# Adding up indexer heads: 128x32 weight matrices on TensorE in place of weighted adds on VectorE and GpSimd

## The chip, the cores and the metric

The kernel is one launch on one core of a Trainium2 chip. The metric is the device time of that launch in microseconds (us); the kernel before ran three times, and its median is 3490.73 us. TensorE (PE) multiplies matrices into the accumulation memory (PSUM); VectorE (DVE), ScalarE (ACT) and GpSimd (POOL) work element by element; SyncE (SP) issues transfers (DMA), which ACT can issue too. Each engine carries out its own instructions in order, and waits for others by semaphores.

## The reference

One decoder layer over 2048 tokens of width 1024. The mixer has two branches that share the input and output projections: sparse attention, whose keys an indexer selects, and an RWKV-7 recurrence. A SwiGLU feed-forward part follows. The change concerns the indexer. Cut to what matters:

```
def block(i):                    # 128 queries
    score = einsum('bth,bths->bts', wi, relu(einsum('bthd,bsd->bths', qi, ik)))   # 8 heads of 64
    score = where(s_pos <= t_pos, score, -inf)
    _, sel = top_k(score, 256)
    ...                          # attention over the selected keys, with a relative bias
```

So for each query and each earlier key, 8 head products go through a relu, are weighted by a number per query and head (`wi`), and are added.

## The kernel before

Four phases follow each other: `phase_in` (projections, to about 769 us), `phase_scan` (to about 1407), `phase_att` (to about 1925) and `phase_ffn`.

`phase_in` works on four groups of 512 tokens. Its function `job` makes the query products of the indexer (`iq`), and of attention (`q`, `k`), as a high and a low half of fp32r, and stores them to DRAM by 256-KB DMAs on SP.

`phase_scan` records two lists of steps into one another. The main list is the RWKV scan: 32 chunks of 64 tokens, for which `load`, `load_t` and `load_r` read matrices from DRAM (BK, ARV, TT, IR), and whose ticks end in an update of the state (L1626, L1627). The side list is the selection (`select_steps`): it takes the query blocks 2 to 15 in five units, (15, 10), (14, 11), (13, 12), (9, 8, 7) and (6, 5, 4, 3, 2). In unit u's span of the scan its scores are made, in u+1's a threshold for the 256 best is searched, in u+2's the mask is written. If a check finds a wrong count, a repair branch runs on DVE. The spans' widths stand in a table (`SPANS`), and each side step gets a position in its span (`at`); a scheduler then orders the instructions of each engine.

The scores of one block are made in pieces of up to 512 keys: 38 pieces in all, 25 of 512 columns, 7 of 384 and 6 of 256. For each piece and each of the 8 heads, `score` multiplies 128 queries of one head by the keys' high half (L933) and low half (L934) into one of two banks `sc`, and ACT takes the relu (L937). Then the heads are added up: head 0 is weighted by POOL into `acc` (L939), head 1 weighted and added by POOL (L941, L942), and heads 2 to 7 each by one DVE instruction (L944):

```
nc.vector.scalar_tensor_tensor(acc[:, ks], r[:, 0:n], w, acc[:, ks], op0=OP.mult, op1=OP.add)
```

`start` loads the indexer's keys `ik` (L873) and weights `iwT` (L876) on SP, ACT and POOL split the keys in two halves (L881, L882), and 16 transposes turn the weights (L885). `others` makes the table of the attention's relative bias: one f32 matmul (L901) gives 8 rows of 384, and one DMA (L911) writes each row 128 times to DRAM (`toep`, 1536 KB). These steps are issued at the scan's start, among the first loads of the scan on SP: `load(0)` (L1529, L1530) ahead of them, the TT loads (L1540, L1541) around them.

Of the kernel before, what the change touches and what calls it, by code (L numbers as in the profile page):

```python
# [144 lines left out]
def phase_in(e, c_in, ada_w, ada_b, x, w_in, pre_gain, q_norm, kv_norm, idx_k_norm,  # L145
# [9 lines left out]
    with ExitStack() as ctx:  # L155
# [289 lines left out]
        def job(g, b, st):  # L445

            gsl = slice(g * G, (g + 1) * G)
            if b in ("iq", "q", "k"):
# [30 lines left out]
            elif b == 3:  # L479
# [4 lines left out]
                nc.sync.dma_start(d.iwT[:, gsl], t[96:104])  # L484
# [325 lines left out]
BESIDE = 2  # L810
# [31 lines left out]
def select_steps(e, pool, psum, ps_, ranks, rel_bias, onehot, d):  # L842
# [19 lines left out]
    iww = pool.tile([P, NB, H], F32, name="iww", bufs=1)  # L862
# [6 lines left out]
    def start():  # L869

        raw = pool.tile([P, UW], F32, name="acc", bufs=3)[:, 0:T]
        for s in (lo, hi):
            nc.sync.dma_start(raw[s], d.ik)  # L873
        wide = pool.tile([P, T], F32, name="xm", bufs=1)
        iwr = wide[0:H]
        nc.sync.dma_start(iwr, d.iwT)  # L876
# [7 lines left out]
        for b in range(NB):  # L884
            nc.tensor.transpose(tp[:, b * H:(b + 1) * H], iwr[:, b * P:(b + 1) * P], e.ident[0:H, 0:H])  # L885
        nc.vector.tensor_scalar(iww.rearrange("p a h -> p (a h)"), tp[:, 0:NB * H], float(8 ** -0.5 * 64 ** -0.5), None, op0=OP.mult)

    def others():
# [22 lines left out]
        nc.sync.dma_start(d.toep, t[:, None, :].to_broadcast([H, P, 384]))  # L911
# [10 lines left out]
    def queries(b):  # L922

        q = pool.tile([P, H, P], F32R, name="iqs", bufs=2)
        for i, s in enumerate((lo, hi)):
            nc.sync.dma_start(f32(q[s]), d.iqT[i, :, b * P:(b + 1) * P].rearrange("(h x) t -> x h t", h=H))
        qs[b] = q

    def score(b, h, o, n):
        acc = accs[b]  # L930
        sp = psum.tile([P, G], F32, name="sc", bufs=2)
        ks = slice(o, o + n)
        nc.tensor.matmul(sp[:, 0:n], qs[b][:, h, :], ikh[:, ks], start=True, stop=False)  # L933
        nc.tensor.matmul(sp[:, 0:n], qs[b][:, h, :], ikl[:, ks], start=False, stop=True)  # L934
        w = iww[:, b, h:h + 1]
        r = pool.tile([P, G], F32, name="relu2", bufs=2) if h < BESIDE else pool.tile([P, G], F32, name="relu", bufs=3)
        nc.scalar.activation(r[:, 0:n], sp[:, 0:n], AF.Relu)  # L937
        if h == 0:
            nc.gpsimd.tensor_tensor(acc[:, ks], r[:, 0:n], w.to_broadcast([P, n]), op=OP.mult)  # L939
        elif h < BESIDE:  # L940
            nc.gpsimd.tensor_tensor(r[:, 0:n], r[:, 0:n], w.to_broadcast([P, n]), op=OP.mult)  # L941
# [1357 lines left out]
```

## Time and profile before

| | us |
|---|---|
| median of 3 runs (lowest, highest) | 3490.73 (3482.89, 3492.33) |
| profiled execution, its span | 3490.94, 3489.2 |
| phase_in: 0 to 769, PE busy | 684.57 |
| gap at the scan's start: 769 to 794, PE busy | 5.07 |
| scores beside the scan: 790 to 1300, PE, DVE, ACT, POOL busy | 421.02, 429.36, 342.59, 259.99 |
| phase_att: 1407 to 1925, PE busy | 480.72 |
| phase_ffn: 1925 to 3489, PE busy | 1510.58 |

PE is busy for 91% of the span, and the phases after the scan are PE's almost alone. The scan stage is the one in which DVE, ACT and POOL have as much to do. A PE record's end is modelled: consecutive matmuls overlap in the records, so the pitch from one start to the next tells what one costs, and not its length. The granted clock (PEclk) is a share of 2.4 GHz.

### The profile page before, as it was taken

Reading aid. Unit: us, or ns where it says so; the run is one execution under the profiler, and the core shown is the slowest. Engines: PE = TensorE matmul, PEld = TensorE weight load, DVE = VectorE, ACT = ScalarE, POOL = GpSimd, SP = SyncE. Lnnn points to the kernel's source line nnn. Section 1 sums busy time; section 2 is a strip of 40 time slices with the busy share of each in tenths; the row PEclk is TensorE's granted clock in tenths of the full one; section 3 lists DMA queues with packets and bytes.
Section 4 is the critical chain, followed back from the end, with each engine's and each line's share of the span. In section 5 each row is a group of like instructions: output and inputs, shape, how many; then the busy total and the mean of one; then the engine's idle time right before and its main releaser. Section 6 shows DMA issues by size and latency. Waiting matters only on the chain.

```text
span 3489.2 us, 47343 instructions
## 1 busy us (share of the span) xinstructions
PE 3186.4 (91%) x15940; PEld 2529.9 (73%) x15940; DVE 2403.5 (69%) x4736; ACT 1758.5 (50%) x3261; POOL 815.4 (23%) x818
## 2 busy tenths in 40 slices
PE   5989999987886898699999898999999989999998
PEld 4666667665675777487877686888887878888886
DVE  5558585765998888488888445786567576656556
ACT  3535353435775776476666443533336443333444
POOL 3545555544554544221110121000000000000000
PEclk8999999987987889799999899999999999999999
DMA  7465747375322343773341477594338653333665
GB/s 203 128 174 140 189 122 214 90 200 114 80 73 69 96 104 98 171 171 85 96 107 39 128 243 272 182 313 138 100 124 291 196 171 109 97 100 109 201 194 194
DMA packets 643431, 516.79 MB, mean 148 GB/s; under 512 B 219520, under 2 KB 509088, under 8 KB 643040
## 3 DMA queue, kind: packets, MB, share of 16 engines
q1 hardware_dynamic: 643176, 513.67, 50.5%
q8 instruction: 126, 2.06, 0.2%
q14 instruction: 129, 1.06, 0.1%
HBM read 355.37 MB, written 158.17 MB: 147 GB/s over the span
## 4 chain that ended last, share of the span: by engine, by line
PE 44%; DVE 5%; DMA 5%; issue 2%; ACT 2%; SPq 1%; POOL 0%; POOLq 0%; DVEq 0%; ACTq 0%
PE b L77 10%; PE b L78 10%; PE b L79 10%; PE pt L1367 3%; PE o L78 2%; PE s L1328 2%; PE o L77 2%; PE o L79 1%; PE s L1329 1%; DMA fb<-hT 1%; PE om L79 1%; DVE wp L1874 1%; PE om L78 1%; PE om L77 1%; DMA fx<-in_w_ffn_down_dram 1%
## 5 line engine op out<-in xcount | busy, mean ns | idle before, releaser
L77 PE MATMUL b<-hT,wp 128*128 128x512 f32 x704 | 276.7, 393 | 4.9 <-ACT wp L1873 3.2
L78 PE MATMUL b<-hT,wp 128*128 128x512 f32 x704 | 276.0, 392 | 0.0
L79 PE MATMUL b<-hT,wp 128*128 128x512 f32 x704 | 275.1, 391 | 0.0
L403 POOL TENSOR_TENSOR wl<-wr,wh 128x512 fp32r<-128x512 f32 (+1 forms) x154 | 203.5, 1338 | 265.6 <-ACT wh L402 260.9
L1873 ACT ACTIVATE wp<-fwr 128x512 fp32r<-128x512 f32 x286 | 177.4, 622 | 165.2 <-PE b L79 91.3
L1874 DVE TENSOR_TENSOR wp<-fwr,wp 128x512 fp32r<-128x512 f32 x286 | 195.9, 686 | 90.9 <-ACT wp L1873 89.7
L77 PE MATMUL b<-wp 128*128 128x512 f32 x616 | 240.1, 390 | 8.5 <-ACT wp L1873 8.5
L78 PE MATMUL b<-wp 128*128 128x512 f32 x616 | 241.7, 392 | 1.7 <-DVE wp L1874 1.4
L77 PE MATMUL mm<-hh,wh 128*128 128x512 f32 (+1 forms) x576 | 241.2, 423 | 1.6 <-ACT wh L402 1.2
L79 PE MATMUL b<-wp 128*128 128x512 f32 x616 | 241.1, 391 | 0.0
L78 PE MATMUL mm<-hl,wh 128*128 128x512 f32 (+1 forms) x576 | 235.0, 408 | 1.3 <-POOL hl L208 1.0
L79 PE MATMUL mm<-hh,wl 128*128 128x512 f32 (+1 forms) x576 | 233.8, 406 | 2.0 <-POOL wl L403 2.0
L1370 ACT ACTIVATE ph<-pt 128x512 fp32r<-128x512 f32 x272 | 158.5, 593 | 123.9 <-PE pt L1367 103.7
L1874 DVE TENSOR_TENSOR wp<-po,wp 128x512 fp32r<-128x512 f32 x154 | 106.3, 691 | 162.5 <-ACT wp L1873 162.4
L1371 DVE TENSOR_TENSOR pl<-pt,ph 128x512 fp32r<-128x512 f32 x272 | 183.9, 687 | 44.3 <-ACT ph L1370 42.9
L77 PE MATMUL b<-hB,wp 128*128 128x512 f32 x528 | 208.4, 395 | 2.5 <-ACT wp L1873 2.5
L79 PE MATMUL b<-hB,wp 128*128 128x512 f32 x528 | 207.9, 394 | 1.5 <-DVE wp L1874 1.5
L78 PE MATMUL b<-hB,wp 128*128 128x512 f32 x528 | 208.1, 394 | 0.0
L944 DVE SCALAR_TENSOR_TENSOR acc<-relu,iww,acc 128x512 f32<-128x512 f32 (+2 forms) x228 | 175.3, 774 | 37.2 <-ACT relu L937 32.0
L937 ACT ACTIVATE relu<-sc 128x512 f32<-128x512 f32 (+2 forms) x304 | 158.3, 542 | 83.0 <-PE sc L934 58.6
L1346 ACT ACTIVATE pr<-pr,nmx 128x1024 f32<-128x1024 f32 (+7 forms) x192 | 171.2, 894 | 55.8 <-DVE nmx L1343 55.3
L933 PE MATMUL sc<-ikh,iqs 128*128 128x512 f32 (+2 forms) x304 | 146.6, 483 | 54.3 <-ACT relu L937 52.2
(504 smaller groups left out, 8459.8 us busy)
## 6 DMA issues: line engine op xcount, KB each, us to landing
wr<-in_w_in_dram SPq DMA_DIRECT2D x63, 512.0 KB, 3.9
fwr<-in_w_ffn_gate_dram SPq DMA_DIRECT2D x44, 512.0 KB, 3.9
fwr<-in_w_ffn_up_dram SPq DMA_DIRECT2D x44, 512.0 KB, 3.9
po<-act_S SPq DMA_DIRECT2D x88, 256.0 KB, 2.7
fwr<-dT SPq DMA_DIRECT2D x88, 256.0 KB, 3.5
act_A<-po SPq DMA_DIRECT2D x66, 256.0 KB, 2.0
act_S<-fb SPq DMA_DIRECT2D x66, 256.0 KB, 2.0
fwr<-in_w_ffn_down_dram SPq DMA_DIRECT2D x66, 256.0 KB, 3.4
```

Of the source, the lines that this page charges most:

```text
L77: nc.tensor.matmul(out, lh, rh, start=first, stop=False, skip_group_check=more)
L78: nc.tensor.matmul(out, lh, rl, start=False, stop=False, skip_group_check=more)
L79: nc.tensor.matmul(out, ll, rh, start=False, stop=last, skip_group_check=more)
L403: nc.gpsimd.tensor_tensor(v(wl), v(wr), f32(v(wh)), op=OP.subtract)
L933: nc.tensor.matmul(sp[:, 0:n], qs[b][:, h, :], ikh[:, ks], start=True, stop=False)
L937: nc.scalar.activation(r[:, 0:n], sp[:, 0:n], AF.Relu)
L944: nc.vector.scalar_tensor_tensor(acc[:, ks], r[:, 0:n], w, acc[:, ks], op0=OP.mult, op1=OP.add)
L1346: nc.scalar.activation(pr[:, 0:w], pr[:, 0:w], AF.Exp, bias=nmx, accum_out=sums[:, i, h:h + 1])
L1370: nc.scalar.activation(ph, tp, AF.Copy)
L1371: nc.vector.tensor_tensor(pl, tp, f32(ph), op=OP.subtract)
L1873: nc.scalar.activation(t[:, 0, :], src, AF.Copy)
L1874: tt(t[:, 1, :], src, f32(t[:, 0, :]), op=OP.subtract)
```

## The change

- **Heads.** `score` now takes 32 queries of 4 heads at a time (128 columns of weights) in place of 128 queries of one head. For a piece there are 2 x 4 such products (a: which four heads; j: which 32 queries), so the count of score matmuls and relus is the same. The adding up is `total`: for each j one f32 matmul of a 128x32 weight matrix (`wts`) with the relu'd scores, into partitions 32j to 32j+31 of a bank `sum`, that is, into one quarter of the array's columns. a = 0 starts the sum, a = 1 ends it: 8 matmuls per piece. DVE copies the bank into `acc`, and adds the causal mask on a block's last 128 columns. `weights` makes the 128x256 weight matrices of a block on DVE. The sum of four heads is issued after the first two scores of the following four.
- **Layout.** The indexer's queries lie in DRAM as [half, 32-token block, 64, head, 32], its weights as [32-token block, head, 32]; stores of `iq` go in runs of 128 B, 16 DMAs per group in place of 8. The halves of `q` and `k` lie in one tile and go by one DMA of 512 KB in place of two. One transpose turns all weights.
- **Queues.** The loads of `start`, `load(0)` and `load_t(0)` are issued from ACT.
- **Bias table.** `bias(h)`: one matmul and one DMA from 128 partitions per head, spread over unit 0 from its 0.6 on.
- **Banks.** The bank `aux` is gone and `sum` takes its place; what used `aux` takes the banks `wk`. `relu` has 6 buffers; the extra tile of the output's squares is gone.

```diff
@@ -454,13 +454,19 @@
                     for k, (sh, sl) in enumerate(src):
                         ws = slice(k * 512 + m * P, k * 512 + (m + 1) * P)
                         mm3(nc, ps, wh[:, ws], wl[:, ws], sh, sl, k == 0, k == len(src) - 1)
-                    out = {"iq": d.iqT, "q": d.qT, "k": d.kT}[b]
                     s = 0.125 if b == "q" else 1.0
-                    h, l = tmp().bitcast(F32R), tmp().bitcast(F32R)
+                    t = pool.tile([P, D], F32, name="xt", bufs=4).rearrange("p (i t) -> p i t", i=2)
+                    h, l = (t[:, i].bitcast(F32R) for i in range(2))
                     nc.scalar.activation(h, ps, AF.Copy, scale=s)
                     nc.vector.scalar_tensor_tensor(l, ps, s, f32(h), op0=OP.mult, op1=OP.subtract)
-                    for i, t in enumerate((h, l)):
-                        nc.sync.dma_start(out[i, m * P:(m + 1) * P, gsl], f32(t))
+                    if b == "iq":
+                        for i in range(2):
+                            for j, rows in enumerate((lo, hi)):
+                                nc.sync.dma_start(d.iq[i, g * 16:(g + 1) * 16, :, 2 * m + j, :].rearrange("b x t -> x b t"),
+                                                  t[rows, i].rearrange("x (b t) -> x b t", t=32))
+                    else:
+                        out = d.qT if b == "q" else d.kT
+                        nc.sync.dma_start(out[:, m * P:(m + 1) * P, gsl].rearrange("i p t -> p i t"), t)
                 return
             ps = product(g, b)
             if b < 3:
...
@@ -870,10 +878,13 @@
 
         raw = pool.tile([P, UW], F32, name="acc", bufs=3)[:, 0:T]
         for s in (lo, hi):
-            nc.sync.dma_start(raw[s], d.ik)
+            nc.scalar.dma_start(raw[s], d.ik)
         wide = pool.tile([P, T], F32, name="xm", bufs=1)
-        iwr = wide[0:H]
-        nc.sync.dma_start(iwr, d.iwT)
+        iwr = wide[:, 0:P]
+        nc.scalar.dma_start(iwr, d.iw.rearrange("b (a h) t -> (b a) (h t)", a=2))
+        nc.vector.tensor_tensor(same, e.ident[:, 0:32], e.ident[:, 32:64], op=OP.add)
+        for q in (2, 3):
+            nc.vector.tensor_tensor(same, same, e.ident[:, 32 * q:32 * q + 32], op=OP.add)
         nc.gpsimd.memset(cm, 0.0)
         nc.gpsimd.affine_select(cm, cm, pattern=[[-1, P]], compare_op=OP.is_ge, fill=BIG, base=0, channel_multiplier=1)
         for g in range(NG):
...
@@ -893,22 +903,25 @@
         nc.vector.tensor_copy(iota8, i8)
         nc.vector.memset(v32, 0.0)
         nc.vector.memset(u32, 0.0)
-        wide = pool.tile([P, H, P], F32R, name="iqs", bufs=2).rearrange("p h t -> p (h t)").bitcast(F32)
-        oh, rb = wide[32:64, 0:384], wide[32:64, 384:384 + H]
-        nc.sync.dma_start(oh, onehot)
-        nc.sync.dma_start(rb, rel_bias)
-        ps = ps_()[0:H, 0:384]
-        nc.tensor.matmul(ps, rb, oh, start=True, stop=True)
-        t = pool.tile([H, G], F32, name="relu", bufs=3)[:, 0:384]
-        nc.scalar.activation(t, ps, AF.Copy)
-        cmb = junk()[:, 0:4 * P].rearrange("p (i t) -> p i t", i=2)
+        t = junk()
+        wide = f32(t)[32:64, 256:]
+        st["oh"], st["rb"] = wide[:, 0:384], wide[:, 384:384 + H]
+        nc.sync.dma_start(st["oh"], onehot)
+        nc.sync.dma_start(st["rb"], rel_bias)
+        cmb = t[:, 0:4 * P].rearrange("p (i t) -> p i t", i=2)
         nc.vector.memset(cmb[:, 0, P:], BIG)
         nc.vector.memset(cmb[:, 1, 0:P], 0.0)
         nc.vector.tensor_copy(cmb[:, 0, 0:P], cm)
         nc.vector.tensor_copy(cmb[:, 1, P:], cm)
         for i in range(2):
             nc.sync.dma_start(d.mask[i][:, 0:2 * P], cmb[:, i, :])
-        nc.sync.dma_start(d.toep, t[:, None, :].to_broadcast([H, P, 384]))
+
+    def bias(h):
+        ps = ps_()[:, 0:384]
+        nc.tensor.matmul(ps, st["rb"][:, h:h + 1].to_broadcast([32, P]), st["oh"], start=True, stop=True)
+        t = pool.tile([P, G], F32, name="relu", bufs=6)[:, 0:384]
+        nc.scalar.activation(t, ps, AF.Copy)
+        nc.sync.dma_start(d.toep[h], t)
 
     accs, qs, st = {}, {}, {}
 
...
@@ -921,29 +934,43 @@
 
     def queries(b):
 
-        q = pool.tile([P, H, P], F32R, name="iqs", bufs=2)
+        q = pool.tile([P, 4, H, 32], F32R, name="iqs", bufs=2)
         for i, s in enumerate((lo, hi)):
-            nc.sync.dma_start(f32(q[s]), d.iqT[i, :, b * P:(b + 1) * P].rearrange("(h x) t -> x h t", h=H))
+            nc.sync.dma_start(f32(q[s]), d.iq[i, 4 * b:4 * b + 4].rearrange("j x h t -> x j h t"))
         qs[b] = q
 
-    def score(b, h, o, n):
-        acc = accs[b]
+    relus, wts, sums = {}, {}, {}
+
+    def score(b, o, n, a, j):
+
         sp = psum.tile([P, G], F32, name="sc", bufs=2)
         ks = slice(o, o + n)
-        nc.tensor.matmul(sp[:, 0:n], qs[b][:, h, :], ikh[:, ks], start=True, stop=False)
-        nc.tensor.matmul(sp[:, 0:n], qs[b][:, h, :], ikl[:, ks], start=False, stop=True)
-        w = iww[:, b, h:h + 1]
-        r = pool.tile([P, G], F32, name="relu2", bufs=2) if h < BESIDE else pool.tile([P, G], F32, name="relu", bufs=3)
+        q = qs[b][:, j, 4 * a:4 * a + 4, :].rearrange("p h t -> p (h t)")
+        nc.tensor.matmul(sp[:, 0:n], q, ikh[:, ks], start=True, stop=False)
+        nc.tensor.matmul(sp[:, 0:n], q, ikl[:, ks], start=False, stop=True)
+        r = relus[b, o, a, j] = pool.tile([P, G], F32, name="relu", bufs=6)
         nc.scalar.activation(r[:, 0:n], sp[:, 0:n], AF.Relu)
-        if h == 0:
-            nc.gpsimd.tensor_tensor(acc[:, ks], r[:, 0:n], w.to_broadcast([P, n]), op=OP.mult)
-        elif h < BESIDE:
-            nc.gpsimd.tensor_tensor(r[:, 0:n], r[:, 0:n], w.to_broadcast([P, n]), op=OP.mult)
-            nc.gpsimd.tensor_tensor(acc[:, ks], r[:, 0:n], acc[:, ks], op=OP.add)
-        else:
-            nc.vector.scalar_tensor_tensor(acc[:, ks], r[:, 0:n], w, acc[:, ks], op0=OP.mult, op1=OP.add)
-        if h == H - 1 and o + n == (b + 1) * P:
-            nc.vector.tensor_tensor(acc[:, o + n - P:o + n], acc[:, o + n - P:o + n], cm, op=OP.add)
+
+    def weights(b):
+        wts[b] = w = pool.tile([P, 4, 2, 32], F32, name="wts", bufs=1)
+        nc.vector.tensor_tensor(w.rearrange("p j a t -> p (j a) t"), wcol[:, 8 * b:8 * b + 8, None].to_broadcast([P, 8, 32]),
+                                same[:, None, :].to_broadcast([P, 8, 32]), op=OP.mult)
+
+    def total(b, o, n, a):
+
+        if a == 0:
+            sums[b, o] = psum.tile([P, G], F32, name="sum", bufs=1)
+        ps, acc = sums[b, o], accs[b]
+        for j in range(4):
+            nc.tensor.matmul(ps[32 * j:32 * j + 32, 0:n], wts[b][:, j, a, :], relus.pop((b, o, a, j))[:, 0:n],
+                             start=a == 0, stop=a == 1)
+        if a == 0:
+            return
+        m = n - P if o + n == (b + 1) * P else n
+        if m:
+            nc.vector.tensor_copy(acc[:, o:o + m], ps[:, 0:m])
+        if m < n:
+            nc.vector.tensor_tensor(acc[:, o + m:o + n], ps[:, m:n], cm, op=OP.add)
 
     def small(name, n=UN, bufs=2):
         return pool.tile([P, n], F32, name=name, bufs=bufs)
...
@@ -1177,7 +1204,9 @@
         nc.vector.scalar_tensor_tensor(mk, eq, BIG, mk, op0=OP.mult, op1=OP.add)
 
     at(0, 0, start)
-    at(0, 0.02, others)
+    at(0, 0.5, others)
+    for h in range(H):
+        at(0, 0.6 + 0.04 * h, bias, h)
     for u, bs in enumerate(UNITS):
         steps = [(space, bs)]
         pieces = []
...
@@ -1187,17 +1216,20 @@
                 pieces.append((b, o, n))
                 o += n
 
-        asked = 0
-        for i in range(-1, len(pieces)):
-            while asked < len(bs) and bs[asked] in {b for b, o, n in pieces[max(i, 0):i + 1 + LEAD]}:
+        asked, late = 0, None
+        for i, (b, o, n) in enumerate(pieces):
+            while asked < len(bs) and bs[asked] in {x[0] for x in pieces[i:i + 1 + LEAD]}:
                 steps.append((queries, bs[asked]))
                 asked += 1
-            now = [(score, pieces[i][0], h, *pieces[i][1:]) for h in range(BESIDE, H)] if i >= 0 else []
-            nxt = [(score, pieces[i + 1][0], h, *pieces[i + 1][1:]) for h in range(BESIDE)] if i + 1 < len(pieces) else []
-            for j in range(max(len(now), len(nxt))):
-                steps += now[j:j + 1]
-                if j % 3 == 0 or not now:
-                    steps += nxt[j // 3:j // 3 + 1] if now else nxt[j:j + 1]
+            for a in range(2):
+                for j in range(4):
+                    steps.append((score, b, o, n, a, j))
+                    if j == 1 and late:
+                        steps.append(late)
+                    if j == 1 and a == 0 and o == 0:
+                        steps.append((weights, b))
+                late = total, b, o, n, a
+        steps.append(late)
         for i, x in enumerate(steps):
             at(u, 0.97 * i / len(steps), *x)
         nb = len(bs)
...
@@ -1522,12 +1554,15 @@
     def ps_():
         return psum.tile([P, 4, P], F32, name="wk", bufs=4)
 
+    def queue(p):
+        return nc.sync if p else nc.scalar
+
     def load(p):
         g, o = p * 2 // GC, p * 2 % GC
         BK = pool.tile([P, 4, 2, 2 * C], F32, name="BK", bufs=2)
         ARV = pool.tile([P, 4, 2, 3 * C], F32, name="ARV", bufs=2)
-        nc.sync.dma_start(BK, d.bk[g][:, :, o:o + 2, :])
-        nc.sync.dma_start(ARV, d.rav[g][:, :, o:o + 2, :])
+        queue(p).dma_start(BK, d.bk[g][:, :, o:o + 2, :])
+        queue(p).dma_start(ARV, d.rav[g][:, :, o:o + 2, :])
         pairs[p] = {"BK": BK, "ARV": ARV}
 
     def load_t(p):
...
@@ -1667,7 +1702,9 @@
             add(gen, ("end", (t - 2) // 2), lambda p=(t - 2) // 2: finish(p))
         if x % 2 == 1 and 0 <= (x + 1) // 2 < NP:
             add(load, (x + 1) // 2)
-        if t % 2 == 1 and 0 <= (t + 3) // 2 < NP:
+            if x < 0:
+                add(load_t, 0)
+        if t % 2 == 1 and 0 < (t + 3) // 2 < NP:
             add(load_t, (t + 3) // 2)
         if 0 <= t + 2 < NC:
             add(load_r, t + 2)
```

The order of TensorE in the scores of unit 0 before. L933 and L934 are the two products of a score (`sc` the bank, `iqs` the queries, `ikh` and `ikl` the keys' halves), L1613 and L1594 are products of the scan:

```order
L933 MATMUL sc<-ikh,iqs 128x512 [waits Activation_49]
L934 MATMUL sc<-ikl,iqs 128x512
L1613 MATMUL wk<-AT,Z_6976 128x128 x2
L933 MATMUL sc<-ikh,iqs 128x512 [waits Activation_49]
L934 MATMUL sc<-ikl,iqs 128x512
L1613 MATMUL wk<-AT,Z_6976 128x128
L933 MATMUL sc<-ikh,iqs 128x384 [waits Activation_49]
L934 MATMUL sc<-ikl,iqs 128x384
L1594 MATMUL wk<-Z_6982,Aa 64x64 [waits DVE_49,PE_49]
L933 MATMUL sc<-ikh,iqs 128x512 [waits Activation_49]
L934 MATMUL sc<-ikl,iqs 128x512
L1594 MATMUL wk<-Z_6982,Aa 64x64 [waits DVE_49]
```

The same stage of the changed program, still in unit 0. L949 and L950 are the score's products, L965 the sums of heads into `sum` (x2: two rows in a run), L1636 and L1648 belong to the scan:

```order
L949 MATMUL sc<-ikh,iqs 128x512
L950 MATMUL sc<-ikl,iqs 128x512
L965 MATMUL sum<-relu,wts 32x512 x2
L1648 MATMUL wk<-AT,Z_6935 128x128 x4
L1636 MATMUL wk<-Z_6929,TT_6943 128x128 x3
L949 MATMUL sc<-ikh,iqs 128x512
L950 MATMUL sc<-ikl,iqs 128x512
L965 MATMUL sum<-relu,wts 32x512
L949 MATMUL sc<-ikh,iqs 128x512
L950 MATMUL sc<-ikl,iqs 128x512
L1636 MATMUL wk<-Z_6929,TT_6943 128x128
```

Pairs of score products still alternate with products of the scan. Sums stand among them in unbroken runs of one to four; four sums that were recorded together are pulled apart by scores. In the whole changed order the 304 sums form 131 runs. A first sum of a piece waits for DVE, which empties the bank.

The first loads of the scan stage on SP before: keys, weights, BK, ARV and queries, and further on the inverses (`TT`) around the bias table (`toep`); `Activation` and `Pool` are engines that an issue waits for, DMAHW an earlier transfer:

```order
L873 DMA acc<-ik 64x2048 [waits DMAHW3_49,PE_49]
L873 DMA acc<-ik 64x2048 [waits DMAHW4_49]
L876 DMA xm<-iwT 8x2048 [waits DMAHW5_49,PE_49]
L1529 DMA BK<-bk_85 128x4x256 [waits DMAHW6_49]
L1530 DMA ARV<-rav_89 128x4x384 [waits DMAHW7_49]
L926 DMA iqs<-iqT 64x8x128 [waits DMAHW0_49]
...
L1540 DMA TT_6985<-inv_109 32x4x64 [waits DMAHW7_49,Pool_49]
L1541 DMA TT_6985<-inv_109 32x4x32 [waits DMAHW0_49]
L1540 DMA TT_6985<-inv_109 32x4x64 [waits DMAHW1_49]
L911 DMA toep<-relu 1024x1x384 [waits DMAHW2_49,Activation_49]
L1541 DMA TT_6985<-inv_109 32x4x32 [waits DMAHW3_49]
```

The same loads on ACT after, behind the last copies of the query product (L460):

```order
L460 ACTIVATE xt<-mm 128x512 [waits DMAHW3_49,DMAHW4_49,DMAHW2_49,DMAHW5_49,DVE_49,PE_49]
L1564 DMA BK<-bk_85 128x4x256 [waits DMAHW3_49,Pool_49]
L1565 DMA ARV<-rav_89 128x4x384 [waits DMAHW5_49]
L881 DMA acc<-ik 64x2048 [waits DMAHW0_49,DVE_49]
L881 DMA acc<-ik 64x2048 [waits DMAHW3_49]
L884 DMA xm<-iw 128x128 [waits DMAHW7_49,DMAHW5_49,Pool_49]
L1575 DMA TT_6938<-inv_109 32x4x64 [waits DMAHW6_49,DMAHW7_49,Activation_49,Pool_49]
L1576 DMA TT_6938<-inv_109 32x4x32 [waits DMAHW1_49]
L892 ACTIVATE ikh<-acc 128x512 [waits DMAHW3_49,DMAHW0_49]
L892 ACTIVATE ikh<-acc 128x512 x3
L952 ACTIVATE relu<-sc 128x512 [waits PE_49]
```

The loads have left SP's order and stand in ACT's, the ones of the scan ahead of those of the indexer, and two TT loads ahead of the cast of the keys (L892), on which the first scores wait. The bias table's DMA is no longer among them; its eight successors come later on SP.

## Rows read from the trace of the kernel before

**Rows 1.** Stretches: window, us, busy us (count) per engine, PEclk, DMA share, GB/s

```profile
769.00:794.00 25.00, 5.07 (x56) 4.47 (x52) 8.99 (x27) 3.69 (x7) 11.59 (x21) 0.58 0.97 250
867.00:1086.00 219.00, 170.50 (x1009) 133.07 (x1008) 198.91 (x462) 141.25 (x254) 107.17 (x151) 0.84 0.27 71
790.00:1300.00 510.00, 421.02 (x2633) 331.49 (x2634) 429.36 (x976) 342.59 (x642) 259.99 (x351) 0.85 0.35 85
1316.00:1349.00 33.00, 31.93 (x306) 28.82 (x304) 31.96 (x104) 28.92 (x61) 17.92 (x38) 1.00 0.40 105
```

**Rows 2.** The page, part 5: line engine op out<-in, shapes xcount | busy, mean ns | idle before

```profile
L1371 DVE TENSOR_TENSOR pl<-pt,ph 128x512 fp32r<-128x512 f32 x272 | 183.9, 687 | 44.3 <-ACT ph L1370 42.9
...
L944 DVE SCALAR_TENSOR_TENSOR acc<-relu,iww,acc 128x512 f32<-128x512 f32 (+2 forms) x228 | 175.3, 774 | 37.2 <-ACT relu L937 32.0
L937 ACT ACTIVATE relu<-sc 128x512 f32<-128x512 f32 (+2 forms) x304 | 158.3, 542 | 83.0 <-PE sc L934 58.6
```

**Rows 3.** PE waits, 790:1302: engine line <- waited for: total us, times, longest

```profile
PE sc L933 <- ACT relu L937: 52.2, 31, 27.5
PE wk L1601 <- DMA TT<-inv: 12.0, 1, 12.0
```

**Rows 4.** Waits of all engines, 1049:1083, same columns

```profile
ACT ajunk L962 <- DVE mk L1177: 28.4, 1, 28.4
```

**Rows 5.** Timeline of PE, 911 to 914: start us, us, engine line op out<-in

```profile
911.23 0.34 PE L933 MATMUL sc<-ikh,iqs 128*128 128x384 f32 x1
911.40 0.34 PE L934 MATMUL sc<-ikl,iqs 128*128 128x384 f32 x1
911.58 0.83 PE L1601 MATMUL wk<-Z,TT 128*128 128x128 f32 x6
912.34 0.40 PE L1647 MATMUL wk<-ident,ysb 64*128 64x64 f32 x3
912.67 0.45 PE L933 MATMUL sc<-ikh,iqs 128*128 128x384 f32 x1
912.95 0.33 PE L934 MATMUL sc<-ikl,iqs 128*128 128x384 f32 x1
913.21 0.53 PE L1647 MATMUL wk<-ident,ysb 64*128 64x64 f32 x5
```

**Rows 6.** Timeline of PE at four places, same columns

```profile
111.98 1.03 PE L430 MATMUL st<-tmp,pick 128*11 128x512 f32 x2
...
768.61 1.15 PE L595 MATMUL mm<-RA,BK 64*64 64x64 f32 x32
...
792.55 1.65 PE L1575 MATMUL wk<-ARV,BK 64*128 64x128 f32 x10
...
1749.30 1.02 PE L138 MATMUL pt<-acc,ones 128*128 128x512 f32 x2
...
1750.38 0.40 PE L1328 MATMUL s<-ks,qh 128*128 128x512 f32 x1
1750.62 0.39 PE L1329 MATMUL s<-ks,ql 128*128 128x512 f32 x1
```

**Rows 7.** DMA issues, 0:800: out<-in queue op xcount, KB each, us to landing

```profile
iqT<-tmp SPq DMA_DIRECT2D x32, 256.0 KB, 2.3
...
inv<-sys SPq DMA_DIRECT2D x6, 256.0 KB, 3.6
```

**Rows 8.** Waits of all engines, 769:800, columns as in rows 3

```profile
ACT ikh L881 <- DMA acc<-ik: 17.6, 1, 17.6
```

**Rows 9.** Timeline of SP's DMA issues at the scan's start, columns as in rows 5

```profile
779.17 1.13 SPq L873 DMA_DIRECT2D acc<-ik  x2
...
799.79 0.80 SPq L911 DMA_DIRECT2D toep<-relu  x1
800.63 9.41 SPq L1541 DMA_DIRECT2D TT<-inv  x1
...
823.42 4.40 SPq L1541 DMA_DIRECT2D TT<-inv  x1
```

More of the change, by code (lines that the diff above doesn't have):

```diff
@@ L483, in job @@
                 nc.scalar.activation(t[96:104], ps[96:104], AF.Copy)
-                nc.sync.dma_start(d.iwT[:, gsl], t[96:104])
+                nc.sync.dma_start(d.iw[g * 16:(g + 1) * 16].rearrange("b h t -> h b t"),
+                                  t[96:104].rearrange("h (b t) -> h b t", t=32))
                 sq = tmp()
@@ L809 @@
 SEARCH = 5
-BESIDE = 2
 LEAD = 3
@@ L861, in select_steps @@
     ikl = pool.tile([P, T], F32R, name="ikl", bufs=1)
-    iww = pool.tile([P, NB, H], F32, name="iww", bufs=1)
+    wcol = pool.tile([P, P], F32, name="wcol", bufs=1)
+    same = pool.tile([P, 32], F32, name="same", bufs=1)
     rk = pool.tile([P, 4, NB - 2], F32, name="ranks", bufs=1)
@@ L883, in start @@
         tp = ps_()
-        for b in range(NB):
-            nc.tensor.transpose(tp[:, b * H:(b + 1) * H], iwr[:, b * P:(b + 1) * P], e.ident[0:H, 0:H])
-        nc.vector.tensor_scalar(iww.rearrange("p a h -> p (a h)"), tp[:, 0:NB * H], float(8 ** -0.5 * 64 ** -0.5), None, op0=OP.mult)
+        nc.tensor.transpose(tp[:, 0:P], iwr, e.ident)
+        nc.vector.tensor_scalar(wcol, tp[:, 0:P], float(8 ** -0.5 * 64 ** -0.5), None, op0=OP.mult)
     def others():
@@ L1539, in load_t @@
                 a, b = 64 * i, 64 * i + 32
-                nc.sync.dma_start(TT[a:a + 32, c, :, a:a + 64], inv[:, 0:32, :].rearrange("h s t -> s h t"))
-                nc.sync.dma_start(TT[b:b + 32, c, :, b:b + 32], inv[:, 32:64, 32:64].rearrange("h s t -> s h t"))
+                queue(p).dma_start(TT[a:a + 32, c, :, a:a + 64], inv[:, 0:32, :].rearrange("h s t -> s h t"))
+                queue(p).dma_start(TT[b:b + 32, c, :, b:b + 32], inv[:, 32:64, 32:64].rearrange("h s t -> s h t"))
     def load_r(x):
@@ L1628, in advance @@
         nc.scalar.activation(ysb[hi, c], ps[hi], AF.Copy)
-        y2 = pool.tile([P, H, 64], F32, name="y2", bufs=1)
-        nc.scalar.activation(y2[hi], ps[hi], AF.Square)
+        y2 = ysb[lo, c]
+        nc.scalar.activation(y2, ps[hi], AF.Square)
         for w in (32, 16, 8, 4, 2, 1):
-            dst = y2[hi, :, 0:w] if w > 1 else var[hi, c, :, None]
-            nc.gpsimd.tensor_tensor(dst, y2[hi, :, 0:w], y2[hi, :, w:2 * w], op=OP.add)
+            dst = y2[:, :, 0:w] if w > 1 else var[hi, c, :, None]
+            nc.gpsimd.tensor_tensor(dst, y2[:, :, 0:w], y2[:, :, w:2 * w], op=OP.add)
     def finish(p):
@@ L1703, in phase_scan, with ps_ @@
         psum = ctx.enter_context(e.tc.tile_pool(name="rw_ps", bufs=4, space=PSUM, reuse_waits="tile"))
-        side = select_steps(e, spool, psum, lambda: psum.tile([P, G], F32, name="aux", bufs=1), ranks,
-                            rel_bias, onehot, d)
+        def ps_():
+            return psum.tile([P, 4, P], F32, name="wk", bufs=4).rearrange("p a n -> p (a n)")
+        side = select_steps(e, spool, psum, ps_, ranks, rel_bias, onehot, d)
         main = [f for steps in scan_steps(e, pool, psum, d) for f in steps]
@@ L1708, in phase_scan @@
         for i, f in enumerate(main):
-            while j < len(side) and side[j][0] * len(main) <= i:
+            while i > 0 and j < len(side) and side[j][0] * len(main) <= i:
                 side[j][1]()
@@ L1712, in phase_scan @@
             f()
-            if i == 0:
-                last = inverse(e, ipool, lambda: psum.tile([P, G], F32, name="aux", bufs=1), NG - 1, d,
+            if i == 1:
+                last = inverse(e, ipool, ps_, NG - 1, d,
                                spool.tile([P, T], F32, name="xm", bufs=1))
@@ L2244, in dram @@
             return dp.tile(shape, dt, name=name)
-        d.ckv, d.ik, d.iwT = dram("ckv", [KV, T]), dram("ik", [64, T]), dram("iwT", [H, T])
-        d.iqT, d.qT, d.kT = dram("iqT", [2, 512, T]), dram("qT", [2, 512, T]), dram("kT", [2, 512, T])
+        d.ckv, d.ik, d.iw = dram("ckv", [KV, T]), dram("ik", [64, T]), dram("iw", [T // 32, H, 32])
+        d.iq, d.qT, d.kT = dram("iq", [2, T // 32, 64, H, 32]), dram("qT", [2, 512, T]), dram("kT", [2, 512, T])
         for n, shape in (("bk", [P, 4, GC, 2 * C]), ("rav", [P, 4, GC, 3 * C]), ("bv", [P, 4, G]),
```

## The prediction

> **What bounds the kernel now.** I read the table of stretches first, then the costliest groups of the page, then TensorE's waits, and last the timelines of single places. In the stretches [rows 1] the reader is to look at two columns, TensorE's (PE) and VectorE's (DVE). The change lies in the stage of the scan, where the indexer's scores run between the steps of the RWKV scan. From 790 to 1300 us DVE is busy for 429.4 of 510 us and PE for 421.0, at a mean granted clock of 0.85. From 867 to 1086 DVE is at 198.9 of 219 (91%) and PE at 170.5 (78%): DVE is the fuller engine. Without scores the same scan runs PE at 31.93 of 33 us with the clock at 1.00, so PE can be filled to 97% there [rows 1].
>
> The DVE work that the change removes is the weighted addition of heads 2 to 7: 228 instructions, 175.3 us [rows 2]. What PE waits for is short. Of 52.2 us behind the activation that empties the score bank, one wait of 27.5 us is most [rows 3]; in that stretch ACT waits 28.4 us for a DVE mask step [rows 4], which is the repair of unit 0's selection. It depends on the scores and not on who adds the heads up, so it stays. Another 12.0 us are a wait for the scan's TT matrices [rows 3], loaded behind the wide bias table on SP [rows 9]. All of PE's idle time is 510 − 421 = 89 us. So the most that can be won by a lighter DVE is 89 − 27.5 = 61.5 us, plus what PE's low clock costs, and against it stands new PE work.
>
> **What is removed.** DVE loses 175.3 us and gets 38 copies of the sum from PSUM (at the 687 ns of the nearest row that reads PSUM at full width [rows 2], at most 26 us) and 14 small weight blocks (under 0.69 us each, so under 10). DVE falls to about 429 − 175 + 36 = 290 of 510. ACT keeps its 304 relus (158.3 us) [rows 2] and its 343 of 510 [rows 1]. GpSimd loses its two heads. None of these binds any more; PE does.
>
> **What is added on PE.** Each of the 38 pieces gets 8 sums: 304 f32 matmuls of 128x32 weights, 200 with 512 columns, 56 with 384, 48 with 256. Each goes twice through the array, as L138's does: two instructions, 1.02 us [rows 6]. The end of a record overlaps what follows: two matmuls of 512 columns start 0.24 us apart and last 0.40 [rows 6], so 0.16 us is tail, and an f32 sum of 512 columns holds the array for 1.02 − 0.16 = 0.86 us. A narrow weight matrix is no cheaper: L430, with 11 columns of weights, takes 1.03 [rows 6]. 384 and 256 columns cost 0.64 and 0.43 in proportion.
> - One after the other: 200 x 0.86 + 56 x 0.64 + 48 x 0.43 = 228 us.
> - All four quarters at once, without a break: 57 us.
> - The order of the changed program breaks the fours up: its 304 sums stand in 131 unbroken runs (93 of 512 columns, of which 37 hold a single sum; 21 of 384; 17 of 256). If a run costs what one sum does: 93 x 0.86 + 21 x 0.64 + 17 x 0.43 = 101 us.
>
> Do quarters overlap? No row of before has four column quarters over the same rows. The nearest: L595's quadrants of 64x64 [rows 6]: 32 in 1.15 us less the tail of 0.16 is 31 ns each, where 64 columns cost 0.86 / 2 / 8 = 54 ns alone. L1575's 10 instructions of 64 rows and 128 columns, at half clock, take 1.65 us [rows 6], while one after the other is 10 x 0.213 = 2.13. Both run two at a time. That is nearest to "a run costs one sum", so I take 101 us and keep 57 and 228 as ends.
>
> The Trainium skill ("TensorE: Matmul & The Clock Gate", Part 3: Packing small matmuls) speaks against it: weight loads go on beside running matmuls only where the row group differs, and column quarters share all rows. By that the sums would be near the 228 us. On full-height matmuls the trace disagrees: the two passes of L138, each with its own weights over the same 128 rows, last 1.02 us with no gap for a load [rows 6]. The same part has three column tiles of 32 gaining 2.38 times, by which a run of three would cost 1.26 sums; no run here shows it.
>
> Each run also changes the shape in which the array is used. A score pair of 384 columns among 128-row matmuls takes 0.35 us (911.23 to 911.58); the same pair between 64-row matmuls takes 0.54 (912.67 to 913.21) [rows 5]. So a change in and out costs 0.19, one about 0.1 us. Counted in the two orders, the changes of form up to 1302 us rise from 262 to 439: 177 x 0.1 = 18 us; 0 if a column quarter isn't such a form. The eight bias matmuls (128x384, f32, 0.64 each, less one before) add 4.
>
> **What PE gets back.** At a mean clock of 0.85 [rows 1], 0.15 x 510 / 0.5 = 153 us run at the lower level of 1.2 GHz. At most the 89 idle ones do no work there, so 64 to 153 busy us do half of what they could: 32 to 76 us return if a denser PE holds 2.4 GHz, as it does at 1316 [rows 1]. I take the middle, 54.
>
> PE then is busy for 421 + 101 + 18 + 4 − 54 = 490 us. At the 97% of the dense stretch that is 505, and with the repair of 27.5 it is 532 in place of 510: **+22 us**. The TT wait of 12.0 is gone in this sum already.
>
> **The start of the scan.** The keys' load is issued at 779.17 by SP [rows 9], and ACT waits 17.6 us for it [rows 8]; from 769 to 794 PE is busy for 5.07 us while the DMA engines are at 0.97 [rows 1]. From ACT's queue the loads go out right behind the last copy of the query product, 7 us earlier: −7, or nothing if the full DMA engines take it back. ACT now also issues the TT loads ahead of the cast of the keys, each waiting for an earlier DMA: up to a few us back. The bias table goes as 8 DMAs from 128 partitions late in unit 0 in place of one from 8 partitions, behind which TT's issues took 9.41 to 4.40 us each [rows 9]; its cost in copies (8 x 0.6 on ACT) is hidden, as ACT has 167 us free.
>
> The Trainium skill ("DMA: Bandwidth & Descriptors", Issuing engines are not separate DMA queues) says that ScalarE's DMAs run on the same 16 engines and only the issue time is saved. The share of 0.97 agrees; by it alone the sum would be 7 us higher.
>
> **The query layout.** Sixteen stores in place of eight per 512 queries, in runs of 128 B. The nearest row with such runs (inv<-sys, 256 KB) lands in 3.6 us against 2.3 for the old store [rows 7]. In the first three groups they lie under phase_in's matmuls and cost nothing. The last group's are issued some twenty DMAs ahead of the scan's first loads, where the engines have no cover left [rows 1]: 8 old stores' worth of 256 KB, 8 x 1.3 = 10 us if the difference in landing is all engine time, 0 if it is delay that overlaps. Below nothing: q and k are stored with half as many issues. I take +5.
>
> **Sum.** 3490.94 + 22 − 7 + 5 = 3511 us, against the profiled execution (span 3489.2 and 1.7 around it), which is 0.2 from the median of the runs.
>
> **Rivals.**
> - *Faster: DVE really was the bound and PE has room.* If entering a column quarter is no change of form and neighbouring runs overlap as well, the sums are 57 us, the changes 0, and a warm PE returns all 76: 421 + 57 + 4 − 76 = 406, / 0.97 + 27.5 = 446, which is 64 less than 510: 3425 us, with the −2 of the start. Half of the way there from my sum is 3468. It decides as soon as the sums with their changes stay under about 100 us in place of my 119 and the clock returns over 60. For it: the DVE row of 91%; against: 37 of the runs hold a single sum, which has no partner.
> - *The passes go in order.* If the second pass of a sum lets only the next sum's first pass start beside it, a run of k costs k + 1 half sums: 164 us in place of 101, 3570 us. Against it: L1575's half rows, above, do better.
> - *The quarters don't overlap*, the skill's rule on weight loads: 228 in place of 101, 3635 us. For it: no row shows same-row quarters. Against: rows 6.
> - *A new wait.* The bank of the sums is single. The first sum of a piece waits until DVE has copied the piece before, and behind it on PE stand the scan's matmuls. PE's relu waits without the repair were 52.2 − 27.5 = 24.7 us [rows 3]; the same again would put 25 us on my sum: 3536.
>
> **How the numbers follow.** My forecast with the new wait as its upper part, 3480 to 3540: 0.47. Faster rival, 3425 to 3480: 0.28. Passes in order, up to 3600: 0.17. No overlap, 3600 to 3650: 0.08. This kernel can tell a change from about 0.3%, 10.5 us: faster is under 3480, slower over 3501. Of my forecast about 0.04 lies under 3480 and 0.18 between. So faster 0.32, same 0.18, slower 0.50 (0.25 of it from my forecast). The forecast's own range is 3480 to 3540; the range for 8 in 10 leaves out no overlap and the lowest of the faster rival: 3445 to 3600.
>
> **What would show it.** The start-to-start times of the sums in one run: 0.01 us with all ending 0.9 later is my case; 0.43 is passes in order; 0.86 no overlap. PE at 95% from 835 us on with a clock near 1.00 except at the repair; DVE under 300 of the stage. PE's wait for TT gone; the first score a few us before 794. A sum that waits for DVE would show the new wait. I am wrong if PE is under 85% there and the stage is shorter: then DVE was what held it. I am also wrong if the phases before 769 or after 1407 change by more than 5 us.

## The result, and the profile after

The changed kernel takes 3531.86 us (median; 3525.78 to 3536.70), the kernel before 3486.81 beside it: a ratio of 1.0127 [1.0103, 1.0152]. It is slower by 45 us. The profiled execution has a span of 3529.0 us against 3489.2, 39.8 more. Three points of the timelines split these 39.8 us: the start of phase_in's last products, the first score, and the last update of the state (L1627 before, L1662 after).

| us | last products of phase_in | first score | last state update | span | gap to the first score | scan stage | the rest |
|---|---|---|---|---|---|---|---|
| before | 769.5 | 794.4 | 1399.4 | 3489.2 | 24.9 | 605.0 | 2089.8 |
| changed | 768.6 | 806.1 | 1433.7 | 3529.0 | 37.5 | 627.6 | 2095.3 |
| changed, once more | 760.1 | 798.1 | 1431.7 | 3520.2 | 38.0 | 633.6 | 2088.5 |

So about 13 us are lost at the scan's start and 23 to 29 in the scan stage. The third row is a second profile of the same kernel: phase_in and the rest differ by 7 to 9 us between the two, and the stage by 6, so differences of that size between single profiles are not explained below.

The stretches of the changed kernel (window, us, then busy us of PE, PEld, DVE, ACT, POOL with counts, granted clock, DMA share, GB/s), which answer to [rows 1]:

```profile
769.00:806.00 37.00, 0.45 (x1) 0.18 (x1) 10.25 (x32) 1.74 (x4) 5.75 (x16) 0.55 0.99 252
806.00:1326.00 520.00, 480.87 (x3212) 299.42 (x3213) 271.63 (x800) 350.61 (x659) 101.15 (x237) 0.96 0.30 82
835.00:1049.00 214.00, 213.65 (x1319) 122.66 (x1319) 101.43 (x329) 157.61 (x278) 36.15 (x99) 1.00 0.28 75
1049.00:1100.00 51.00, 19.64 (x111) 11.13 (x112) 38.50 (x63) 12.09 (x26) 0.94 (x1) 0.70 0.12 39
```

Beside the scores TensorE is busy for 480.87 of 520 us at a clock of 0.96, VectorE for 271.63: the fuller engine is the other one now. From 835 to 1049 us TensorE is busy for 213.65 of 214 us at a clock of 1.00; the 51 us behind that hold the repair. The sums alone (L965, 600 of their 608 instructions; PE and PEld busy, clock, DMA share, GB/s):

```profile
806.00:1326.00 520.00, 126.88 (x600) 19.13 (x600) 0.96 0.30 82
```

The waits of TensorE from 800 to 1326 us, which answer to [rows 3] and [rows 8]:

```profile
PE wk L895 <- DMA xm<-iw: 35.8, 1, 35.8
PE sc L949 <- ACT relu L952: 35.7, 8, 31.2
PE sc L949 <- DVE g L1032: 2.4, 1, 2.4
```

The 12.0 us for TT are gone, the repair's wait is there with 31.2 us, and hardly anything else is. The long one at the top lies ahead of the first score: the indexer's weights come late.

The sums on TensorE's timeline (start us, us, then instructions; x2 is one f32 sum in two passes, x6 three sums):

```profile
904.74 0.40 PE L950 MATMUL sc<-ikl,iqs 128*128 128x512 f32 x1
905.07 1.05 PE L965 MATMUL sum<-relu,wts 128*32 128x512 f32 x2
906.04 0.71 PE L1610 MATMUL wk<-ARV,BK 64*128 64x128 f32 x6
...
911.26 1.05 PE L965 MATMUL sum<-relu,wts 128*32 128x512 f32 x2
912.24 0.50 PE L949 MATMUL sc<-ikh,iqs 128*128 128x512 f32 x1
912.57 0.40 PE L950 MATMUL sc<-ikl,iqs 128*128 128x512 f32 x1
912.90 1.06 PE L965 MATMUL sum<-relu,wts 128*32 128x512 f32 x6
913.89 0.32 PE L1661 MATMUL st<-state,Q 128*128 128x64 f32 x1
```

From its own start to the next instruction's a run of one sum takes 0.97 us (905.07 to 906.04) and a run of three 0.99 (912.90 to 913.89). The quarters do run at the same time, and a run costs what one sum does. The score ahead of it holds the array for 0.33 us (904.74 to 905.07) where 0.24 is its pitch among its like [rows 6]: 0.09 us to enter. To leave is 0.97 − 0.86 = 0.11, an estimate, since 0.86 was the prediction's own for the two passes. The first score behind a run takes 0.33 as well (912.24 to 912.57), which neither figure counts.

At the start, SP's issues of the changed kernel:

```profile
757.04 14.33 SPq L465 DMA_DIRECT2D iq<-xt  x16
...
779.75 3.74 SPq L469 DMA_DIRECT2D qT<-xt  x4
```

and the same two steps of the kernel before:

```profile
756.01 5.58 SPq L463 DMA_DIRECT2D iqT<-tmp  x8
...
769.88 5.29 SPq L463 DMA_DIRECT2D qT<-tmp  x8
```

From the first to the last, sixteen stores of 128-B runs take SP 14.33 us, eight of 2-KB rows 5.58. In both stretches there are pauses between the issues; one issue by itself takes 0.66 us after and 0.39 before (number of them, shortest, median and longest in ns, first and last start in us):

```profile
L465 SPq DMA_DIRECT2D iq<-xt x64: 574/660/1420, 215.4 to 770.7; - x64
```

```profile
L463 SPq DMA_DIRECT2D iqT<-tmp x32: 319/388/724, 209.0 to 761.3; - x32
```

Are full DMA engines what holds SP up here? While it issues the sixteen their share is lower than in the same stretch before (before, then after; columns as above):

```profile
757.00:772.00 15.00, 12.41 (x77) 8.88 (x75) 8.00 (x13) 5.48 (x9) 3.19 (x3) 1.00 0.91 273
```

```profile
757.00:772.00 15.00, 11.81 (x75) 8.72 (x73) 10.47 (x14) 4.59 (x8) 2.91 (x3) 1.00 0.78 132
```

So the length is SP's own, 16 x 0.66 = 10.6 us of it by the issues alone; in the three groups of tokens before, the sixteen take 12.5 to 14.2 us. The stores of q are issued behind them, 9.9 us later than before. What ACT does then:

```profile
774.12 0.60 ACT L460 ACTIVATE xt<-mm 128x512 fp32r<-128x512 f32 x1 [2.33 <-DMA iq<-xt]
787.89 0.62 ACTq L1564 DMA_DIRECT2D BK<-bk  x1
788.59 0.59 ACTq L1565 DMA_DIRECT2D ARV<-rav  x1
789.37 3.05 ACTq L881 DMA_DIRECT2D acc<-ik  x2
796.87 0.36 ACTq L884 DMA_DIRECT2D xm<-iw  x1
803.56 0.32 ACTq L1575 DMA_DIRECT2D TT<-inv  x1
805.04 0.31 ACTq L1576 DMA_DIRECT2D TT<-inv  x1
805.45 2.19 ACT L892 ACTIVATE ikh<-acc 128x512 fp32r<-128x512 f32 x4 [30.74 <-DVE wcol L896]
```

ACT is done with the query product at 774.7, its copies having waited for stores of iq, but issues its first load at 787.89 (in the order this load waits for GpSimd, which waits 24.0 us for a store of q). The keys' load goes out at 789.37, where SP issued it at 779.17 before [rows 9].

### The profile page after: what moved, and what is told of

Read it like the earlier page. It is cut to its first block, busy times and chain, and to the rows that moved or that the text cites. A ratio compares the mean times of both kernels' runs of the same rounds, so it can differ in the third digit from the quotient of the medians.

```text
span 3529.0 us, 47918 instructions
## 1 busy us (share of the span) xinstructions
PE 3248.6 (92%) x16547; PEld 2500.3 (71%) x16547; DVE 2244.1 (64%) x4563; ACT 1766.3 (50%) x3270; POOL 659.2 (19%) x704
## 3 DMA queue, kind: packets, MB, share of 16 engines
q14 instruction: 125, 1.02, 0.1%
## 4 chain that ended last, share of the span: by engine, by line
PE 45%; DVE 5%; DMA 4%; ACT 2%; issue 2%; SPq 1%; POOL 0%; POOLq 0%; DVEq 0%; ACTq 0%
PE b L77 10%; PE b L78 10%; PE b L79 10%; PE pt L1399 3%; PE o L78 2%; PE s L1360 2%; PE o L77 2%; PE s L1361 1%; PE o L79 1%; PE om L79 1%; PE om L78 1%; PE om L77 1%; DMA fx<-in_w_ffn_down_dram 1%; PE pt L1425 1%; DMA fb<-hT 1%
## 5 line engine op out<-in xcount | busy, mean ns | idle before, releaser
L1912 ACT ACTIVATE wp<-po 128x512 fp32r<-128x512 f32 x154 | 96.8, 629 | 187.5 <-PE b L79 149.7
L402 ACT ACTIVATE wh<-wr 128x512 fp32r<-128x512 f32 (+1 forms) x154 | 93.7, 620 | 167.9 <-PE mm L78 77.4
```

The source lines that it names most:

```text
L402: nc.scalar.activation(v(wh), v(wr), AF.Copy)
L1912: nc.scalar.activation(t[:, 0, :], src, AF.Copy)
```

## The experiments

All medians stand beside 3489.5 to 3490.0 us of the kernel before on the same chip. "Below the changed kernel" means below its 3531.86; beside these runs it measured 3529.37, by which each such difference is 2.5 us smaller.

**Sums in fours.** The same kernel, only the order in which a group's four sums are written:

```diff
-        for j in range(4):
+        for j in (3, 2, 1, 0):
             nc.tensor.matmul(ps[32 * j:32 * j + 32, 0:n], ...
```

> The changed kernel with one edit: the four sums of a group are written in the order j = 3, 2, 1, 0, so the first of them needs the last relu, and all 304 sums then stand in 76 runs of four in place of 130 broken ones. Theory 1 (TensorE holds the stage, and a run costs what its longest column of quarters costs, 0.86 us at 512 columns, plus a change of form in and out of 0.2 us): the runs fall from 100 to 57 us, and 54 changes in and out fall away, 54 x 0.2 = 11 us, so 3532 - 54 = 3478 us, the scan's start and the later phases as they were. Theory 2 (the stage is held by the chain of scores, relus and the scan, and the sums lie beside it): no change, 3532 within 8 us. Theory 3 (grouping makes TensorE wait for the last relu of a group): slower, TensorE's wait for relus over 50 us.

Measured: 3475.15 us (3465.02 to 3479.96), a ratio to the kernel before of 0.9944 [0.9921, 0.9967]. That is 57 us below the changed kernel, where 54 were expected, and faster than the kernel before. The scan stage falls from 627.6 to 577.8 us. A run of four on its timeline, with its weight loads (PEld):

```profile
831.13 0.40 PE L950 MATMUL sc<-ikl,iqs 128*128 128x512 f32 x1
831.45 0.16 PEld L965 LDWEIGHTS sum<-relu,wts 128*32 128x32 f32 x8 [0.36 <-issue]
831.46 1.06 PE L965 MATMUL sum<-relu,wts 128*32 128x512 f32 x8
832.45 0.50 PE L949 MATMUL sc<-ikh,iqs 128*128 128x512 f32 x1
```

Four sums take the 0.99 us that three take, 0.02 more than one. The weights of all eight passes are loaded within 0.16 us, beside running matmuls. All sums by line (instructions, then busy us, mean ns), of the changed kernel and then of this one:

```profile
L965 PE MATMUL sum<-relu,wts 128*32 128x512 f32 (+2 forms) x608 | 128.4, 560 | 0.0
```

```profile
L965 PE MATMUL sum<-relu,wts 128*32 128x512 f32 (+2 forms) x608 | 73.8, 557 | 0.4 <-ACT relu L952 0.3
```

54.6 us less for the same 608 instructions, and the wait for the last relu of a group, which theory 3 feared, is 0.3. TensorE holds the stage (theory 1).

**Queries in rows of 2 KB.** `iq` is stored as q and k are, and the load cuts it up:

```diff
-                    if b == "iq":
-                        for i in range(2):
-                            for j, rows in enumerate((lo, hi)):
-                                nc.sync.dma_start(d.iq[...])
...
+                    out = {"iq": d.iqT, "q": d.qT, "k": d.kT}[b]
+                    nc.sync.dma_start(out[:, m * P:(m + 1) * P, gsl]..., t)
...
+            for j in range(4):
+                nc.sync.dma_start(f32(q[s, j]), d.iqT[i, :, b * P + 32 * j:b * P + 32 * j + 32]...)
```

> The changed kernel with one edit: the indexer's queries are stored as before, in rows of 2 KB, by one DMA of 512 KB for both halves as q and k are, and the load cuts them into 32 tokens (8 DMAs per block in place of 2). Theory 1 (SP's 14.3 us for sixteen stores of 128-B runs put the scan's start off): SP issues the q stores some 10 us earlier, the first score comes 8 to 12 us earlier, and the time is 3532 - 10 = 3522 us. Theory 2 (the loads on ScalarE's queue put it off, since they wait for GpSimd and for earlier transfers in front of the cast of the keys): no change at the start, 3532 us. Theory 3 (the DMA engines are full either way): the q stores go out earlier but land as late, 3532 us.

Measured: 3520.60 us (3514.01 to 3526.86), ratio 1.0078 [1.0053, 1.0102]: 11 below the changed kernel, 10 expected. The gap to the first score is 28.6 us in place of 37.5. SP's issues:

```profile
755.59 3.40 SPq L463 DMA_DIRECT2D iqT<-xt  x4
...
768.55 3.76 SPq L463 DMA_DIRECT2D qT<-xt  x4
...
777.60 16.83 SPq L934 DMA_DIRECT2D iqs<-iqT  x16
```

The stores take 3.40 us and q's go out at 768.55, 11.2 us earlier. The sixteen loads that replace them, 16.83 us of issues, stand behind the stores of q; what they cost there was not measured apart. The edit makes issues and transfers coarser at once, so it does not part the two by itself; but with q's stores 11.2 us earlier the first score does come earlier, against theory 3, and the DMA share above was lower while SP issued the sixteen. SP's issue time at this place was the price (theory 1).

**First loads on SP.** `nc.scalar.dma_start` becomes `nc.sync.dma_start` in `start`, and `queue(p)` returns `nc.sync`:

```diff
-            nc.scalar.dma_start(raw[s], d.ik)
+            nc.sync.dma_start(raw[s], d.ik)
...
-        return nc.sync if p else nc.scalar
+        return nc.sync
```

> The changed kernel with one edit: the first loads of the scan (keys, weights, BK, ARV, TT of the first pair) are issued by SP again. Theory 1 (SP is the late one at the start, by its sixteen stores): the loads come behind still more on SP, and the time is the same or up to 5 us longer, 3532 to 3537 us. Theory 2 (ScalarE's queue with its waits puts the start off): the first score comes 8 to 13 us earlier, 3522 us.

Measured: 3509.72 us (3506.17 to 3510.99), ratio 1.0053 [1.0031, 1.0075]: 22 us below the changed kernel. By the number that is theory 2, but its reason isn't there: the gap to the first score is 37.6 us, as in the changed kernel (37.5 and 38.0), and the waits are as long:

```profile
PE wk L895 <- DMA xm<-iw: 34.5, 1, 34.5
ACT ikh L892 <- DMA acc<-ik: 28.3, 1, 28.3
POOL amask L1521 <- DMA qT<-xt: 23.8, 1, 23.8
```

What is shorter is the stretch from the first score to the first state update, 75.7 us against 84.8, and there the scheduler's order is another: 23 runs of sums in place of 27, which at 0.98 us each are 4 us, and 190 products of the scan in place of 204, so 14 of them come later. So both theories were wrong on this run, the first on its number, the second on its place. Of the 22 us I can place some 10 in the scan stage (617.6 us against 627.6); the rest lies where two profiles of one kernel differ as much, and its cause stays open.

**Both edits**, sums in fours and rows of 2 KB:

> The edits of the first two runs together: sums in fours, and the queries stored in rows of 2 KB. Theory 1: both gains add up, since one is in the scan stage and one ahead of it: 3532 - 54 - 10 = 3468 us, 19 less than the kernel before. Theory 2: what is won at the start is lost again later, or the scan is held by another engine once the sums are in fours: 3490 us or more.

Measured: 3462.14 us (3455.23 to 3463.94), ratio 0.9909 [0.9887, 0.9930]. The gains add up: 70 us below the changed kernel, 64 expected. The gap is 30.5 us, the scan stage 576.4.

**All three edits.**

> Sums in fours, queries stored in rows of 2 KB, and the first loads issued by SP: the three edits of the runs before together. Where the gain of the loads on SP (22 us, of which the trace shows nothing between the end of phase_in and the first score, 37.6 us against 37.5) came by the other order of the sums in unit 0 (23 runs in place of 27 ahead of the first state update), it is gone once all sums stand in fours: 3462 us, within 6. Where it is the queue itself, it adds up: 3440 to 3445 us.

Measured: 3458.63 us (3446.96 to 3459.47), ratio 0.9915 [0.9897, 0.9933]. With the sums in fours nothing clear is left of the 22 us of the queue. The profile is of the fastest execution, 3446.96 us, the other three lying at 3458.41 to 3459.47; in it the gap is 26.5 us and the stage 570.5, so that a gain of a few us at the start is neither shown nor excluded. This and the run before it are the fastest versions, 27 to 31 us under the kernel before; which of the two is faster these runs don't tell.

**The changed kernel again.**

> The changed kernel as it is, beside the other runs of this chip: whether 3532 us holds on it. If the comparison with the loads on SP is a matter of the chip, it comes out near 3515; if not, 3526 to 3537.

Measured: 3529.37 us (3521.90 to 3532.34), ratio 1.0120 [1.0100, 1.0140]. The result stands; the chip was not the reason for the run on SP.

**The kernel before with the bias table late.** `others` at 0.5, and `bias(h)` as the change has it, nothing else (cut to where they are placed):

```diff
-    at(0, 0.02, others)
+    at(0, 0.5, others)
+    for h in range(H):
+        at(0, 0.6 + 0.04 * h, bias, h)
```

> The kernel before with one part of the change: the bias table late in unit 0, as eight matmuls and eight DMAs from 128 partitions. Theory 1 (the stage of before is held by more than that stall): the wait of 12.0 us for TT goes, and with DVE nearly full behind it 4 to 12 us of it remain as gain: 3489 - 8 = 3481 us. Theory 2 (the stall was slack that the later stage absorbs): 3489 within 3. Theory 3 (eight more f32 matmuls and copies in a full stage cost what the stall gave): 3489 or a little more.

Measured: 3477.49 us (3475.62 to 3483.59), ratio 0.9972 [0.9961, 0.9982]: 12.5 us less by the medians, 6 to 14 by the ratio. The gap is 25.8 us, the scan stage 589.7 in place of 605.0. Waits of TensorE and the stretch of the scores:

```profile
PE sc L936 <- ACT relu L940: 61.3, 33, 31.7
PE aux L885 <- DMA xm<-iwT: 18.8, 1, 18.8
PE wk L1618 <- DVE Aa L1584: 5.5, 4, 3.1
```

```profile
790.00:1290.00 500.00, 415.11 (x2674) 323.06 (x2676) 431.46 (x983) 348.12 (x655) 264.31 (x351) 0.88 0.34 88
```

The wait for TT is gone, and ahead of the first state update nothing took its place: from the first score to that update it is 59.8 us in place of 72.4. Behind it waits for relus grow, 61.3 us in all against 52.2 [rows 3], at a clock of 0.88 against 0.85 [rows 1], and the stage keeps its gain. The 12.0 us were no slack (theory 1): the stage moves up by them, with VectorE still at 431 of 500.

## Why the prediction was right

The forecast was 3511 us, slower, with 3445 to 3600 as the range; 3532 came. The mechanism is the forecast one, TensorE's new work in the scan stage:
- *A run costs one sum.* This was the choice on which the sum stood. Runs of one, three and four take 0.97 to 0.99 us from their start to the next instruction's. In the trace the first passes of a run start 0.01 us apart, as the prediction wanted of its case, and the second passes 0.45 us behind the first ones. The two rivals on this point, passes in order and no overlap, are refuted by those rows. (By their own terms they come to 3511 + 63 = 3574 and 3511 + 127 = 3638 us, not 3570 and 3635; no range hangs on it.) The Trainium skill's rule on weight loads ("TensorE: Matmul & The Clock Gate", Part 3: Packing small matmuls) does not hold here for column quarters over the same rows: in the run of four all eight loads lie within 0.16 us, beside running matmuls over those rows. By the estimate that the prediction took from the Trainium skill's three column tiles (same part, 2.38 times), a run of three costs 1.26 sums; it is 0.99 / 0.97 = 1.02.
- *Changes of form.* 0.1 us each way: 0.09 to enter as measured, 0.11 to leave as estimated, with the longer score behind a run left out.
- *The clock.* 0.96 on the mean, 1.00 from 835 to 1049, 0.70 in the repair.
- *TensorE's total.* The sum had it busy for 490 us; it is 480.87. Two terms were off against each other. The sums' records fill 126.88 us where 101 were counted; some 9 us of that are the records' tails (130 runs, 1.05 against 0.98 each), and part is the leaving, which the prediction has in its 18. All else on TensorE is 354 us between the first score and the last, where it was 414.03 before (the row below, columns as in [rows 1]): 60 us less, where the prediction had −54 + 18 + 4 = −32. The clock can give back at most half of the time no longer spent at the lower level, (0.14 × 501 − 0.04 × 520) / 0.5 / 2 = 49 us. What made the rest shorter no run here shows. That the total came so near is partly luck.

```profile
794.40:1295.70 501.30, 414.03 (x2598) 325.71 (x2598) 426.09 (x969) 339.26 (x635) 255.29 (x346) 0.86 0.34 84
```

- *VectorE* under 300: 271.63.
- *The stage.* +22 us was forecast for the stretch of the scores. From the first score to the last it is 500.8 us before and 520.1 after, 523.0 in the second profile: +19 and +22. To the last state update it is +22.6, and +28.6 in the second profile. The waits that a single bank of sums might bring did not come: no sum waits for VectorE. That rival's 3536 lies nearer to the measured time than 3511 by chance.
- *The faster rival* fell on its own condition: the sums with their changes had to stay under about 100 us, and the sums' records alone are 128.4. That it was near, the first experiment shows: in fours they are 73.8 with 54 fewer entries and exits, and the kernel is faster than before.

The step that failed is the start of the scan. "−7, or nothing" for the loads on ScalarE and "I take +5" for the query layout make −2; measured are +12.6, and the first score comes at 806.1 and not a few us before 794. The layout was priced by how long a store takes to land and not by what sixteen issues take on SP, 14.33 us in place of 5.58, with everything behind them moved: the stores of q, GpSimd's clearing that waits for one of them, and ScalarE's loads that wait for GpSimd. The second experiment gives back 8.9 us of the gap by that alone. And the loads on ScalarE brought nothing there: they went out behind the store of q that GpSimd waited for, and with them on SP the gap is the same. These 14.6 us are most of the 21 between forecast and result.

One sign of being wrong was set too fine: a change of more than 5 us ahead of 769 or behind 1407. The rest is 5.5 us longer in the first profile and 1.3 shorter in the second, phase_in 0.9 and 9.4 shorter; one kernel differs from itself by more than the sign allows, so it tells nothing.

The gain of the bias table was counted inside the stage's sum. Alone it makes the stage 589.7 us, so what the sums of heads add to a stage free of that stall is more like 38 to 44 us (627.6 and 633.6 against 589.7, single profiles). The other parts of the change, the banks and the single transpose of the weights among them, were not run apart.

## What to carry to other kernels

Matmuls that share the array pay only while they stand side by side: look at the order in which a scheduler leaves them and count the unbroken runs, not the matmuls. Writing first the one that becomes ready last kept four together here and was worth 54 to 57 us. And price a store that is cut finer by the issuing queue's time as well as by its bytes, with all that is queued behind it.

## What the runs showed that was not expected

- Four f32 sums of 128x32 in the four column quarters take 0.99 us, a single one 0.97: with two passes each, the four first passes start within 0.02 us, and the four second ones 0.45 us later.
- On SP a store of 128-B runs from 64 partitions takes 0.66 us to issue (median of 64), one of 2-KB rows 0.39 (median of 32). With twice as many of them and the pauses between, that made 14.33 us out of 5.58.
- Moving first loads from one queue to another changed the order of the sums far away from them (27 runs to 23). In the profile the time moved there, and not in the gap that the loads were meant to shorten.
